# VectorE's passes in the order of their description in the FFN, and one more 7-product pair in the first group of each second product

## The chip, the cores and the metric

The kernel runs on one core of one Trainium2 chip. The metric is the device time of one execution in microseconds (us), the median of several runs. The engines' names are those of the profile: PE is the matrix engine (TensorE), PEld its weight loads, DVE is VectorE, ACT is ScalarE, POOL is GpSimd, SP the engine that issues most DMAs.

## The reference

One layer of a residual block on 256 tokens of width 2048, all in float32. The change is in the FFN, the second of three parts:

```python
merged = (sigmoid(gate_sb) * (y_sb @ w_sb_out) + sigmoid(gate_ca) * (y_ca @ w_ca_out))
x = x + merged @ w_mix_out
h = rmsnorm(x, g_ffn)
g_ff, u_ff = split(h @ w_ffn_in, 2, axis=-1)        # 2048 x 11264
x = x + (silu(g_ff) * u_ff) @ w_ffn_out             # 5632 x 2048
h = rmsnorm(x, g_ple)
x = x + sigmoid(h @ w_ple_gate) * (p @ w_ple_in)
return rmsnorm(x, g_final)
```

## The kernel before

**Every product is three products.** PE multiplies in a reduced form of float32 (`F32R`). To keep float32's precision, each operand is split: `hi` is the operand rounded, `lo` the rest, and a product is the sum of `hi*hi`, `hi*lo` and `lo*hi` (`three`, L307). Activations are split once into tables (T1, T2, T3). Weights come from memory into a `raw` buffer (128 x 1024 float32, two rows of blocks of 128 x 512); ACT casts `raw` to `hi` (L277) and DVE subtracts, `lo = raw - hi` (`minus`, L257). There are three `hi` and three `lo` buffers, a fourth of each in the FFN. PE reads them, and when its last matmul on a buffer is over, ACT may cast the next piece into it.

**Units, groups and pieces.** A *unit* computes two column groups of 512 columns side by side, with two token tiles each: four PSUM banks. Its work is cut into pieces along the contraction, two blocks of 128 rows each. A piece of one group has 12 matmuls, so both groups' pieces of the same rows have 24. Alternatively a pair of rows is done for both groups at once by a scheme with seven products in place of eight (`split_pair`, `pair_products`): 21 matmuls. The weights' sums that it needs are made of the two raw buffers by DVE (four passes of 128 x 512 into `xf` and `raw`), split by ACT (L292, L295, L298) and DVE (two `lo` passes and one of 128 x 1536). The sums of the activations come from `table_part` and `sums_of`: ACT copies the transposed tile to `af` (L496) and casts it (L500), DVE makes four small sums `fm` (L466, L257), ACT casts them (L470), DVE makes the rest.

**Which pairs, in which order.** A tuple lists a unit's pieces: a number twice is a pair of rows done plainly (one piece for each group), a negative number a 7-product pair.

```python
OUT_PAIRS = {12: (2, 3, 4), 16: (2, 4, 5, 6)}
OUT_ORDERS = {
    12: ((0, 0, 1, 1, -2, 3, 3, -4, 5, 5), (0, 0, -2, 1, -3, 1, -4, 5, 5)),
    16: ((0, 0, 1, 1, -2, 3, 3, -4, 5, 5, -6, 7, 7), (0, 0, 1, -2, 1, -4, 3, -5, 3, -6, 7, 7)),
}
```

**The FFN.** The hidden width 5632 is done in three blocks of 12, 16 and 16 tiles of 128 (blocks 0, 1, 2 below). In each block the first product (`w_ffn_in`) runs as 3, 4 and 4 units, each making 512 hidden columns; then the second product (`w_ffn_out`) runs as two units, `c = 0` (columns 0 to 1023 of x) and `c = 2` (1024 to 2047). The document calls them the first and second out unit; the change's title calls the units' pairs of columns groups. After each unit DVE adds the sums of the 7-product pairs (`mid`, L854), adds the banks (`add_sums`, L858; `add_to_sums`, L1066), multiplies (L1059), and a later task turns the result into a table (`into_table`: PE transposes L482, then `table_part`).

**Between the mixers and the FFN** the RMS norm's scale is only known after all of x: `norm`, `halve_rstd` and `broadcast` (L137, PE L139, DVE copy L140) make `p2bc`, and from then on `scale_next` multiplies each tile of T3 by it (`scale_table`, L821) after the tile's last use without it, and makes the sums for its pairs (`pair_sums`, L842). At the end of the FFN the tables for the last part are made with a gain (L508 on ACT, L509 on DVE).

**What sets the order.** `flush` goes through the pieces: `prefetch` describes the DMA and the splits of up to three pieces ahead, `products` the matmuls and what follows them, then a task. That is the order of description. The program is then put in order by a scheduler that simulates all engines: on each engine it takes what it finds ready, so the engines' queues differ from the order of description. The queues are fixed when the program is built, and an instruction that waits in one holds those that stand behind it.

Of the kernel before, what the change touches and what calls it, by code (L numbers as in the profile page):

```python
# [38 lines left out]
# [4 lines that stand above are left out]
# [10 lines left out]
def block_kernel(ctx: ExitStack, tc: tile.TileContext, x, p, w_in, w_sb_out, w_ca_out, w_mix_out,  # L53
# [100 lines left out]
    def run_task():  # L154
        name, fn = tasks.popleft()
        fn()
        if name is not None:
            done.add(name)
# [15 lines left out]
    def unit(wsrc, n0s, kts, lhs, forms, ext, slots, mid, post, needs, row0=0, pairs=PAIRS, alone=None, after=None,  # L174
             order=None, seed=None):


        if alone is None:
            state["unit"] = state.get("unit", -1) + 1
        pool = state["unit"] % 2 if alone is None else alone  # L180
        g = dict(kind="unit", post=post, mid=mid, slots=slots, after=after, lhs=lhs, keep=None, forms=forms, ext=ext, pool=pool,
                 side=1 - pool, hold=alone is not None, seed=seed)
        kts = list(kts)
        if order is None:
            order = [j for i in range(len(kts) // 2) for j in ([-i] if i in pairs and i < len(kts) // 2 - 1 else [i, i])]
        taken = [-i for i in order if i < 0]
        begun = set()
        for i in order:
            own = i < 0
            i = abs(i)  # L190
            part = kts[2 * i : 2 * i + 2]
            r = (row0 + 2 * i) * P
            src = [wsrc[r : r + 2 * P, n0 : n0 + NB].rearrange("(k p) n -> p k n", p=P) for n0 in n0s]
            pc = dict(g=g, kts=part, ncol=NB, needs=[needs(kt) for kt in part])
            if own:
                pieces.append(dict(pc, src=src, pair=True, first=i == taken[0], last=i == taken[-1]))
            else:
                b = int(i in begun)
                begun.add(i)
                pieces.append(dict(pc, src=[src[b]], block=b, first=i == 0, last=2 * i + 2 == len(kts)))  # L200
# [139 lines left out]
    def seed_next():  # L340

        pc = pieces[min(state["at"] + 2, len(pieces) - 1)]
        g = pc["g"]
        if g.get("seed") is not None and "ps" not in g:
            for b in range(2):
                open_sums(g)
                for t in range(2):
                    nc.scalar.copy(g["ps"][2 * b + t], g["seed"](b, t))

    def products(pc):  # L350
        g = pc["g"]
        if pc.get("pair"):
            pair_products(pc)
        elif g["kind"] == "unit":
            if pc["first"] and g["seed"] is None:
                open_sums(g)
            for i, kt in enumerate(pc["kts"]):
                a, z = pc["first"] and i == 0 and g["seed"] is None, pc["last"] and i == 1
                for t in range(2):
                    row_products(g["ps"][2 * pc["block"] + t], g["lhs"], kt, t, pc["hi"][:, i, :], pc["lo"][:, i, :], a, z)  # L360
            if g["after"] is not None and pc["block"] == 1:
                g["after"](pc["kts"])
            if pc["last"]:
                g["post"](g, pc["block"])
                state["hold"] = g["hold"] and pc["block"] == 0
        elif pc is pieces[1]:
            with tc.issue_after(state["mm"].ins):
                group_products(pc)
        else:
            group_products(pc)  # L370
        del pc["hi"], pc["lo"]
# [36 lines left out]
    def prefetch():  # L408
        while state["loaded"] < len(pieces) and state["raw"] + len(pieces[state["loaded"]]["src"]) <= RAW + state["places"]:
            load(pieces[state["loaded"]])  # L410
            state["loaded"] += 1
        room = 2 if state["at"] < 4 + KD // 2 else 4 if state["fourth"] is not None else 3
        while state["split"] < state["loaded"] and state["split"] <= state["at"] + 3:
            pc = pieces[state["split"]]
            if state["split"] > state["at"] and sum(map(size, pieces[state["at"] : state["split"] + 1])) > room:
                break
            behind = [started["p"]]
            if pc["g"] is pieces[4]["g"]:
                behind += started.get(pc["kts"][0] - 2, [])
            with ExitStack() as order:  # L420
                for i in behind:
                    order.enter_context(tc.issue_after(i.ins))
                split(pc)
            state["split"] += 1
# [11 lines left out]
    def flush(every=1, until=None, in_turn=False):  # L436

        n = 0
        while state["at"] < len(pieces) and (until is None or until not in done):
            pc = pieces[state["at"]]  # L440
            prefetch()
            products(pc)
            seed_next()
            state["at"] += 1
            n += 1
            if tasks and every and not state["hold"] and int(n / every) > int((n - 1) / every):
                if in_turn:
                    with tc.issue_after(state["mm"].ins):
                        run_task()
                else:  # L450
                    run_task()
# [547 lines left out]
    def rooms(t):  # L999
        return [t.rearrange("p k c s -> p (k c s)")[:, o : o + 3072] for o in (0, 3072)]  # L1000
# [42 lines left out]
    def out_form(pairs):  # L1043
        return lambda kt: late["F"][1][pairs.index(kt // 2)]
# [23 lines left out]
    def residual_of(c0):  # L1068
        return lambda b, t: x_[:, t, (c0 + b) * NB : (c0 + b + 1) * NB]

    def out_unit_post(c0, last):
        def post(g, b):
            if last and c0:
                if b == 0:
                    return
                with tc.issue_after(pieces[state["at"] + 3]["split"].ins):
                    for b in range(2):
                        add_to_sums(g, b, c0 + b)
                        residual_done(c0 + b, "ple")
                next_tables(T1, c0 + b, 32, "ple", g["pool"])  # L1080
                done.add("ffn end")
                return
            add_to_sums(g, b, c0 + b)
            if last:
                if b == 1:
                    next_tables(T1, c0 + b, 32, "ple", g["pool"])
                residual_done(c0 + b, "ple")
        return post

    k0 = 0  # L1090
    for blk, nk in enumerate(FF_BLOCKS):
        key = f"h{blk}"
        for c in range(nk // 4):
            j = k0 // 4 + c
            unit(w_ffn_in[0], (j * NB, D_FF + j * NB), range(KD), T3, lambda kt: late["F"][0][kt // 4 - 1], rooms(T1),
                 C_slots, mid, (in_post if j else first_post)(T2, c, key, OUT_PAIRS[nk]), lambda kt: ("ffn", kt),
                 pairs=PAIRS if j else (), after=None if j else scale_next)
        last = blk == len(FF_BLOCKS) - 1
        for c in (0, 2):
            unit(w_ffn_out[0], (c * NB, (c + 1) * NB), range(nk), T2, out_form(OUT_PAIRS[nk]), rooms(T3 if last else T1),  # L1100
                 C_slots, mid, out_unit_post(c, last), lambda kt, key=key: (key, kt), row0=k0,
                 order=OUT_ORDERS[nk][c // 2], seed=residual_of(c))
        k0 += nk

    pins, ple = {}, {}
# [83 lines left out]
        group("row", w_ple_gate[0], c * NB, range(KD), T1, ple_post(c), needs=pneed)  # L1189
    group("row", w_ple_gate[0], 3 * NB, range(KD), T1, last_post, needs=pneed, keep=keep)  # L1190
    state["ps"] = late["ps"][state["unit"] % 2 == 0]
    flush(until="ffn end")

    ple["pi"] = lp.tile([P, 2, NT, NB], F32, tag="C", name="pi")
    gf = ple["gf"] = lp.tile([P, D], F32, tag="gf", name="gf")
# [26 lines left out]
```

## Time and profile before

| | |
|---|---|
| median of 3 runs | 1456.49 us (1455.96 to 1457.09) |
| the profiled execution | 1455.66 us, its span 1453.9 us |
| granted TensorE clock, mean | 0.998 |
| the mixers' out products end, mix units | about 600 to 660 us |
| FFN: first products of block 0, 1, 2 | about 660 to 797, 857 to 1027, 1109 to 1279 us |
| FFN: second products of block 0, 1, 2 | about 797 to 857, 1027 to 1109, 1279 to 1359 us |
| last part and end | 1359 to 1454 us |

The stages' bounds are those at which the passes that end a unit (L966, L1059, L1066) stand in the trace. In rows of the timeline the columns are start, length, engine, line, operation, out<-in and count, then the idle time before it and what ended that. `T` stands for any of the tables, since buffer numbers are left out.

### The profile page before, as it was taken

How to read it: one execution, taken by the hardware profiler on the slowest of the kernel's cores; microseconds unless marked ns; L12 is line 12 of the kernel's file. 1: busy time of each engine (PE TensorE's matmuls, PEld its weight loads, DVE VectorE, ACT ScalarE, POOL GpSimd, SP SyncE). 2: the span in 40 equal slices, each digit the busy share in tenths (PEclk: the TensorE clock that was granted, in tenths of full speed). 3: DMA queues.
4: the chain of work that ended last, by engine and by line, in shares of the span. 5: the costliest groups of instructions: out<-in, count | busy, mean ns of one | idle time of the engine just before them, and what ended most of it. 6: DMA issues, size and time to landing. Idle time of an engine off the chain costs nothing.

```text
span 1453.9 us, 18702 instructions
## 1 busy us (share of the span) xinstructions
PE 1443.5 (99%) x6837; PEld 1208.8 (83%) x6837; DVE 1249.7 (86%) x1587; ACT 829.6 (57%) x993; POOL 25.1 (2%) x44
## 2 busy tenths in 40 slices
PE   9999999999999999999999999999999999999997
PEld 7888888888888888888888888888888888888886
DVE  6979777898987767888999999999999989999785
ACT  6456555655545665555556655566655556666652
POOL 0200000000010000000000000000000000000100
PEclk9999999999999999999999999999999999999999
DMA  9866555666675655765666666666666666665871
GB/s 319 283 189 212 181 172 172 180 205 198 199 257 164 180 168 181 231 204 173 198 192 189 196 222 194 199 201 208 193 194 216 195 186 201 215 189 178 275 230 70
DMA packets 164731, 291.17 MB, mean 200 GB/s; under 512 B 9024, under 2 KB 42096, under 8 KB 164384
## 3 DMA queue, kind: packets, MB, share of 16 engines
q1 hardware_dynamic: 162528, 281.32, 62.0%
q0 software_dynamic: 2112, 8.68, 1.8%
q8 instruction: 53, 0.87, 0.2%
q14 instruction: 38, 0.31, 0.1%
HBM read 284.19 MB, written 5.77 MB: 199 GB/s over the span
## 4 chain that ended last, share of the span: by engine, by line
PE 96%; DVE 2%; DMA 1%; issue 1%; ACT 0%; DVEq 0%; SPq 0%; ACTq 0%
PE mm L307 67%; PE su L307 13%; PE mm L392 8%; PE mm L394 4%; PE tp L482 1%; DVE lo L257 1%; DMA raw<-in_w_in 1%; PE mml L307 0%; DMA raw<-in_w_ple_in 0%; PE mm L382 0%; PE xps L536 0%; DVE xf L257 0%; PE yp L709 0%; ACT hi L277 0%; PE wt L800 0%
## 5 line engine op out<-in xcount | busy, mean ns | idle before, releaser
L307 PE MATMUL mm<-hi,T 128*128 128x512 f32 x2650 | 854.6, 391 | 0.4 <-DVE v L854 0.4
L257 DVE TENSOR_TENSOR lo<-raw,hi 128x1024 fp32r<-128x1024 f32 (+1 forms) x517 | 625.1, 1221 | 121.9 <-ACT hi L277 113.0
L277 ACT CAST hi<-raw 128x1024 fp32r<-128x1024 f32 (+1 forms) x379 | 396.7, 1050 | 381.0 <-PE mm L307 257.8
L307 PEld LDWEIGHTS mm<-hi,T 128*128 128x128 f32 x2650 | 497.3, 188 | 103.0 <-issue 0.8
L307 PE MATMUL mm<-lo,T 128*128 128x512 f32 x1325 | 517.1, 391 | 0.0
L307 PEld LDWEIGHTS mm<-lo,T 128*128 128x128 f32 x1325 | 248.9, 188 | 50.7
L392 PE MATMUL mm<-T,hi 128*128 128x512 f32 x512 | 179.8, 398 | 0.0
L394 PE MATMUL mm<-T,lo 128*128 128x256 f32 x512 | 139.7, 280 | 0.0
L295 ACT CAST hi<-raw 128x1024 fp32r<-128x1024 f32 x69 | 72.7, 1053 | 76.2 <-DVE raw L257 29.5
L257 DVE TENSOR_TENSOR T<-xf,T 128x1536 fp32r<-128x1536 f32 x61 | 107.2, 1757 | 8.0 <-ACT T L298 7.2
L392 PEld LDWEIGHTS mm<-T,hi 128*128 128x128 f32 x512 | 94.6, 188 | 20.1
L257 DVE TENSOR_TENSOR xf<-raw 128x512 f32<-128x512 f32 x138 | 95.1, 689 | 13.2 <-DMA raw<-in_w_ffn_out 4.1
L394 PEld LDWEIGHTS mm<-T,lo 128*128 128x128 f32 x512 | 96.7, 189 | 2.3
L298 ACT CAST T<-xf 128x1536 fp32r<-128x1536 f32 x61 | 90.2, 1479 | 12.7 <-DVE xf L257 12.3
L292 ACT CAST hi<-raw 128x1024 fp32r<-128x1024 f32 x69 | 72.6, 1052 | 31.0 <-PE mm L307 20.5
L307 PE MATMUL mm<-T,T 128*128 128x512 f32 (+1 forms) x279 | 77.2, 371 | 0.0
L307 PE MATMUL su<-hi,T 128*128 128x512 f32 x170 | 66.1, 394 | 0.0
L307 PEld LDWEIGHTS mm<-T,T 128*128 128x128 f32 x279 | 49.3, 188 | 9.1
L854 DVE TENSOR_TENSOR C<-su,C 128x512 f32<-128x512 f32 x72 | 47.8, 686 | 0.4
L257 DVE TENSOR_TENSOR xf<-raw,xf 128x512 f32<-128x512 f32 x69 | 47.5, 689 | 0.5
L257 DVE TENSOR_TENSOR raw<-raw 128x512 f32<-128x512 f32 x69 | 47.5, 689 | 0.4
L307 PE MATMUL su<-T,FP 128*128 128x512 f32 x174 | 47.3, 389 | 0.0
(280 smaller groups left out, 1242.7 us busy)
## 6 DMA issues: line engine op xcount, KB each, us to landing
raw<-in_w_ffn_in SPq DMA_DIRECT2D x176, 512.0 KB, 4.1
raw<-in_w_in SPq DMA_DIRECT2D x160, 512.0 KB, 4.4
raw<-in_w_ffn_out SPq DMA_DIRECT2D x88, 512.0 KB, 4.4
raw<-in_w_mix_out SPq DMA_DIRECT2D x32, 512.0 KB, 4.6
raw<-in_w_ple_gate SPq DMA_DIRECT2D x32, 512.0 KB, 4.9
raw<-in_w_sb_out SPq DMA_DIRECT2D x16, 512.0 KB, 3.8
raw<-in_w_ca_out SPq DMA_DIRECT2D x16, 512.0 KB, 4.5
x<-in_x SPq DMA_DIRECT2D x4, 512.0 KB, 10.2
```

Source lines behind the costliest of these rows:

```text
L257: return nc.vector.tensor_tensor(out, a, b, ALU.subtract)
L277: state["cast"] = nc.scalar.copy(hi[:, c : c + m], raw[:, c : c + m])
L292: nc.scalar.copy(h1, raw1)
L295: nc.scalar.copy(h2, raw2)
L298: nc.scalar.copy(xh, xf)
L307: state["mm"] = nc.tensor.matmul(ps, u, v, start=first, stop=last, skip_group_check=True)
L392: nc.tensor.matmul(ps, hi[:, i, f], lhs[:, kt, :, :].rearrange("p c s -> p (c s)"), start=a, stop=False)
L394: nc.tensor.matmul(ps[:, :S], lo[:, i, f], lhs[:, kt, 0, :], start=False, stop=z)
L482: nc.tensor.transpose(ps[:, k, t * P : (t + 1) * P], src[:, t, (k0 + k) * P : (k0 + k + 1) * P], ident)
L854: nc.vector.tensor_tensor(C[i], q, C[j], ALU.add)
```

## The change

Two edits. The first out unit of each block takes the tuple that the second has, with one 7-product pair more (three in place of two in block 0, four in place of three in blocks 1 and 2). And DVE's queue is kept in the order of description from the last pieces before the FFN to the task that ends it; PE, ACT, POOL and SP are still ordered by the scheduler.

```diff
             unit(w_ffn_out[0], (c * NB, (c + 1) * NB), range(nk), T2, out_form(OUT_PAIRS[nk]), rooms(T3 if last else T1),
                  C_slots, mid, out_unit_post(c, last), lambda kt, key=key: (key, kt), row0=k0,
-                 order=OUT_ORDERS[nk][c // 2], seed=residual_of(c))
+                 order=OUT_ORDERS[nk][1], seed=residual_of(c))
...
-    flush(until="ffn end")
+    with tc.manual_schedule(engines={mybir.EngineType.DVE}):
+        flush(until="ffn end")
```

PE has 9 matmuls of 128 x 512 fewer; DVE has 12 passes of 128 x 512 and 3 of 128 x 1536 more; ACT has 3 casts of 128 x 1536 more.

**Place 1: DVE where the FFN's norm becomes known.** `T` is T3, `lo` the rest of a weight piece, `fm` the small sums. Before:

```order
L140 COPY p2bc<-rps 128x256
L821 TENSOR_TENSOR T_5123<-T_5123,p2bc 128x2x256 x3
L257 TENSOR_TENSOR lo<-raw,hi 128x1024
L821 TENSOR_TENSOR T_5123<-T_5123,p2bc 128x2x256 x3
L257 TENSOR_TENSOR lo<-raw,hi 128x1024
L821 TENSOR_TENSOR T_5123<-T_5123,p2bc 128x2x256 x2
L842 TENSOR_TENSOR af<-T_5123 128x512
L257 TENSOR_TENSOR lo<-raw,hi 128x1024
```

Now, on the same engine and at the same place:

```order
L140 COPY p2bc<-rps 128x256
L257 TENSOR_TENSOR lo<-raw,hi 128x1024 x2
L821 TENSOR_TENSOR T_5123<-T_5123,p2bc 128x2x256 x6
L842 TENSOR_TENSOR af<-T_5123 128x512
L466 TENSOR_TENSOR fm<-af 128x128
L257 TENSOR_TENSOR fm<-af 128x128
L257 TENSOR_TENSOR fm<-fm,af 128x128
L257 TENSOR_TENSOR fm<-af,fm 128x128
L257 TENSOR_TENSOR FP<-fm,FP 128x512
L821 TENSOR_TENSOR T_5123<-T_5123,p2bc 128x2x256 x2
L257 TENSOR_TENSOR lo<-raw,hi 128x1024 x2
```

Where a `lo` pass stood after at most three scalings, eight scalings and a pair's sums stand now between the second and the third `lo` pass. On ACT, the casts of the sums (L470 into FP, for which DVE's FP passes wait) stood apart before, the second of them behind three more casts of weights. They stand together now, still behind six casts of weights, each of which waits for PE to free its buffer:

```order
L508 ACTIVATE T_5123<-tp,gT 128x256
L277 CAST hi<-raw 128x1024 x6
L470 CAST FP<-fm 128x512 x2
L277 CAST hi<-raw 128x1024 x3
L1036 ACT_TABLE_LOAD
```

**Place 2: the table of two pairs in a first product.** This is the last unit but one of blocks 1 and 2 and the last of block 0. `T_72` is T2's part, `af` the transposed tile, `fm` its sums, which end in T1's room and in F_more. DVE before, from the first table's rest to the second's end:

```order
L257 TENSOR_TENSOR T_71<-fm,T_71 128x512
L257 TENSOR_TENSOR xf<-raw 128x512
L257 TENSOR_TENSOR T_72<-af,T_72 128x2x256
L257 TENSOR_TENSOR lo<-raw,hi 128x1024
L466 TENSOR_TENSOR fm<-af 128x128
L257 TENSOR_TENSOR fm<-af 128x128
L257 TENSOR_TENSOR raw<-raw 128x512
L257 TENSOR_TENSOR lo<-raw,hi 128x1024
L257 TENSOR_TENSOR fm<-fm,af 128x128
L257 TENSOR_TENSOR xf<-raw 128x512
L257 TENSOR_TENSOR lo<-raw,hi 128x1024
```

DVE now:

```order
L257 TENSOR_TENSOR T_71<-fm,T_71 128x512
L257 TENSOR_TENSOR T_72<-af,T_72 128x2x256
L466 TENSOR_TENSOR fm<-af 128x128
L257 TENSOR_TENSOR fm<-af 128x128
L257 TENSOR_TENSOR fm<-fm,af 128x128
L257 TENSOR_TENSOR fm<-af,fm 128x128
L257 TENSOR_TENSOR F_more<-fm,F_more 128x512
L257 TENSOR_TENSOR lo<-raw,hi 128x1024 x2
```

And ACT now, at the same place; the second row waits for a matmul that is 19 matmuls ahead of the first that reads DVE's next `lo`:

```order
L277 CAST hi<-raw 128x1024
L292 CAST hi<-raw 128x1024
L470 CAST T_71<-fm 128x512
L496 COPY af<-tp 128x512
L500 CAST T_72<-af 128x2x256
L470 CAST F_more<-fm 128x512
```

DVE's three `lo` passes inside the table's work have moved behind it, and DVE's first row waits for ACT's third, which stands behind two casts of weights.

**Place 3: DVE at the start of block 0's first out unit.** The banks `mm` of the last unit of the first product are added and multiplied (L858, L1059), and the first pair of the out unit is made (`xf`, `raw`, `T_71`; the table's rest is `T_72<-af`). Before:

```order
L858 TENSOR_TENSOR C<-mm_6505,C 128x512
L858 TENSOR_TENSOR C<-mm_6521,C 128x512
L858 TENSOR_TENSOR C<-mm_6520,C 128x512
L257 TENSOR_TENSOR lo<-raw,hi 128x1024
L257 TENSOR_TENSOR T_71<-xf,T_71 128x1536
L257 TENSOR_TENSOR lo<-raw,hi 128x1024
L1059 SCALAR_TENSOR_TENSOR C<-C,r_ffn 128x512 x2
L257 TENSOR_TENSOR xf<-raw 128x512
L257 TENSOR_TENSOR lo<-raw,hi 128x1024 x2
L257 TENSOR_TENSOR raw<-raw 128x512
L257 TENSOR_TENSOR lo<-raw,hi 128x1024
L257 TENSOR_TENSOR xf<-raw 128x512
```

Now:

```order
L858 TENSOR_TENSOR C<-mm_6523,C 128x512
L1059 SCALAR_TENSOR_TENSOR C<-C,r_ffn 128x512 x2
L257 TENSOR_TENSOR xf<-raw 128x512
L257 TENSOR_TENSOR raw<-raw 128x512
L257 TENSOR_TENSOR xf<-raw 128x512
L257 TENSOR_TENSOR xf<-raw,xf 128x512
L257 TENSOR_TENSOR lo<-raw,hi 128x1024 x2
L257 TENSOR_TENSOR T_71<-xf,T_71 128x1536
L257 TENSOR_TENSOR lo<-raw,hi 128x1024
L257 TENSOR_TENSOR T_72<-af,T_72 128x2x256
L466 TENSOR_TENSOR fm<-af 128x128
L257 TENSOR_TENSOR fm<-af 128x128
```

The `lo` passes that stood among L1059 and the pair's four sums have moved behind them, in twos.

## The prediction

> **What bounds the kernel now.** First the page's busy times and its chain of work that ended last:
>
> ```profile
> PE 1443.5 (99%) x6837; PEld 1208.8 (83%) x6837; DVE 1249.7 (86%) x1587; ACT 829.6 (57%) x993; POOL 25.1 (2%) x44
> PE 96%; DVE 2%; DMA 1%; issue 1%; ACT 0%; DVEq 0%; SPq 0%; ACTq 0%
> ```
>
> PE is the bound and stands still almost nowhere. So a matmul saved is worth its full time, and a wait put into PE costs its full time too. The second view is the busy time by stretch of the FFN (columns: bounds, length, then busy us and count of PE, PEld, DVE, ACT, POOL, then the granted clock, DMA's share, GB/s). The stretches are block 0's end of the first product and its out units, then block 1's out units:
>
> ```profile
> core 0: us, PE busy (x) PEld busy (x) DVE busy (x) ACT busy (x) POOL busy (x), PEclk, DMA share, GB/s
> 795.00:825.00 30.00, 30.00 (x138) 24.84 (x137) 28.51 (x38) 20.29 (x24) 0.00 (x0) 1.00 0.62 196
> 825.00:857.00 32.00, 32.00 (x143) 26.52 (x142) 30.91 (x36) 15.54 (x16) 0.00 (x0) 1.00 0.61 200
> 984.00:1027.00 43.00, 43.00 (x196) 35.71 (x195) 41.47 (x55) 27.68 (x32) 0.00 (x0) 1.00 0.63 195
> 1027.00:1066.00 39.00, 39.00 (x177) 32.32 (x176) 36.09 (x45) 24.47 (x28) 0.00 (x0) 1.00 0.63 193
> ```
>
> PE is busy in every microsecond, and DVE has only 3 to 7% of these stretches free. The third view, the waits by kind (idle us, count, longest), tells which way the engines lead each other:
>
> ```profile
> ACT hi L277 <- PE mm L307: 257.8, 156, 6.7
> DVE lo L257 <- ACT hi L277: 113.0, 118, 2.4
> ```
>
> ACT waits until PE frees a `hi` buffer, then casts, and DVE follows on its heels. How far they run ahead of PE is therefore set by the three or four buffers: a wait inside DVE's queue can last until the next `lo` is due on PE, and no longer.
>
> **The change part by part.** I take start-to-start times ("pitch") from the timeline. PE's matmul, first and last of five starts in a row:
>
> ```profile
> 805.48 0.39 PE L307 MATMUL mm<-hi,T 128*128 128x512 f32 x1
> ...
> 806.39 0.39 PE L307 MATMUL mm<-hi,T 128*128 128x512 f32 x1
> ```
>
> (806.39 - 805.48) / 4 = 0.227 us. *What is saved:* three more 7-product pairs make 21 matmuls of 24 each, 9 fewer: 9 x 0.227 = **-2.04 us**, on the path.
>
> *What is added* is 12 DVE passes of 128x512 and 3 of 128x1536, and three casts of 128x1536 on ACT. DVE's pitches, from back-to-back passes near block 1's end:
>
> ```profile
> 990.82 0.29 DVE L466 TENSOR_TENSOR fm<-af 128x128 f32<-128x128 f32 x1
> 991.02 0.28 DVE L257 TENSOR_TENSOR fm<-af 128x128 f32<-128x128 f32 x1
> ...
> 995.16 1.76 DVE L257 TENSOR_TENSOR T<-xf,T 128x1536 fp32r<-128x1536 f32 x1
> 996.83 1.22 DVE L257 TENSOR_TENSOR lo<-raw,hi 128x1024 fp32r<-128x1024 f32 x1
> 997.97 0.69 DVE L257 TENSOR_TENSOR T<-fm,T 128x512 fp32r<-128x512 f32 x1
> 998.57 0.69 DVE L257 TENSOR_TENSOR xf<-raw 128x512 f32<-128x512 f32 x1
> ```
>
> That is 0.20 us for a `fm`, 1.67 for 128x1536, 1.14 for a `lo`, 0.60 for 128x512. So 12 x 0.60 + 3 x 1.67 = 12.2 us of DVE work are added, 4.1 in each first out unit. These stretches have 1 to 3 us of DVE free each, so the cover is about gone. ACT's pitches, and the hops between engines:
>
> ```profile
> 993.24 1.48 ACT L298 CAST T<-xf 128x1536 fp32r<-128x1536 f32 x1
> 995.00 1.06 ACT L277 CAST hi<-raw 128x1024 fp32r<-128x1024 f32 x1 [0.28 <-PE mm L307]
> 995.95 0.62 ACT L470 CAST T<-fm 128x512 fp32r<-128x512 f32 x1
> 996.47 0.58 ACT L496 COPY af<-tp 128x512 f32<-128x512 f32 x1
> 997.08 0.62 ACT L500 CAST T<-af 128x512 fp32r<-128x512 f32 x1
> ```
>
> ```profile
> 806.66 0.29 DVE L257 TENSOR_TENSOR fm<-af,fm 128x128 f32<-128x128 f32 x1
> 806.98 0.63 ACT L470 CAST F_more<-fm 128x512 fp32r<-128x512 f32 x1
> 808.43 0.39 PE L307 MATMUL mm<-hi,T 128*128 128x512 f32 x1
> 808.86 1.06 ACT L277 CAST hi<-raw 128x1024 fp32r<-128x1024 f32 x1 [1.25 <-PE mm L307]
> ```
>
> A weight cast takes 0.95, L470 0.52, L496 to L500 0.61; DVE's last sum to ACT's cast 0.03; from the start of PE's last matmul on a buffer to ACT's cast into it 0.43.
>
> *What is moved* is the large part. In the order of description, DVE may meet a pass whose input ACT makes only behind a cast that waits for PE, while PE soon needs the `lo` behind that pass. For each such loop I add up the way from PE's releasing matmul through ACT and DVE to the `lo`, and compare it with the matmuls that PE has until it needs that `lo`. What is over is PE's idle time. In before's order no loop is that tight, in accord with PE's full stretches.
>
> **A, the norm (Place 1).** Before, its rows are
>
> ```profile
> 674.82 0.60 PE L139 MATMUL rps<-dg,ones 128*128 128x256 f32 x2
> ...
> 675.46 0.42 DVE L140 COPY p2bc<-rps 128x256 f32<-128x256 f32 x1 [0.81 <-PE rps L139]
> ...
> 675.92 1.90 DVE L821 TENSOR_TENSOR T<-T,p2bc 128x512 fp32r<-128x512 f32 x3
> ...
> 677.73 1.22 DVE L257 TENSOR_TENSOR lo<-raw,hi 128x1024 fp32r<-128x1024 f32 x1
> ...
> 678.87 1.89 DVE L821 TENSOR_TENSOR T<-T,p2bc 128x512 fp32r<-128x512 f32 x3
> ```
>
> From the broadcast's start, L140 begins at 0.64 and takes 0.46; the `lo` behind it ends at 2.33, and PE needs it after its two broadcasts and four matmuls, at 1.58: 0.8. Then come a `lo` (1.14), six scalings (6 x 0.60), L842 (0.60) and the `fm` (0.80), to 8.4; the cast of FP (L470), which on ACT stands behind a weight cast that is released at 7.1 + 0.43, starts at 8.5 and ends at 9.1; FP's pass, two scalings and the `lo` end at 12.2. PE wants that `lo` at 7.8: 4.4. The next pair of rows, with the same steps but fewer scalings, lacks 0.8. Together **+6.0**.
>
> **B, the two-pair tables (Place 2), three times:** 0.43 + weight cast 0.95 + L470 0.52 + L496 0.61 + L500 and hop 0.65 + DVE's T pass 0.60 + four `fm` 0.89 + hop 0.03 + L470 and hop 0.65 + F pass 0.60 + `lo` and hop 1.26 = 7.2 us, against 19 matmuls, 4.3. PE stands 2.9 us, so **+8.6**.
>
> **C, the start of the out units (Place 3).** In block 0, from the sums that end the first product (four L854) to the next pair's `lo` DVE has 32 passes: 19 of 128x512 (11.4), two L1059 (0.66 each, 1.3), six `lo` (6.8), one of 1536 (1.7), four `fm` (0.8), in all 22.0. PE has 89 matmuls and 8 transposes of 0.11 for them, 21.1. With PE's start (0.35), the wait for the cast of F_more (0.9) and the hop (0.1), 2.3 is over, and another 0.3 by the second out unit. The casts of this unit, `hi`, 128x1536 and then DVE's 128x1536 (4.7 us against 16 to 19 matmuls, 3.6 to 4.3), lack 0.9, 0.4 and 0.6: 4.5 for block 0. The same account gives 3.2 for block 1, whose table comes with fewer sums, and 1.5 for block 2: **+9.2**.
>
> **D, the gain tables in block 2's second out unit:**
>
> ```profile
> L508 ACT ACTIVATE T<-tp,gT 128x256 fp32r<-128x256 f32 x32 | 13.6, 475 | 6.8 <-DVE T L509 5.2 <-PE tp L482 1.6
> L509 DVE SCALAR_TENSOR_TENSOR T<-tp,gT,T 128x256 fp32r<-128x256 f32 x32 | 14.0, 483 | 0.5 <-ACT T L508 0.4
> ```
>
> Now DVE's eight L509 stand together ahead of the next pair's sums, and between ACT's last L508 there are two weight casts, each waiting for PE. Each way, 0.43 + 0.95 + L508 0.51 + L509 0.52 = 2.4, stands against 8 and then 4 matmuls (1.8, 0.9): 0.6 + 1.5. The next pair's four sums and `lo`, 6.0 us after the second release, are wanted after 9 matmuls and the stall, at 3.5: 2.4. **+4.5**. **E**, one-pair tables of the units between: 0.2 twice, **+0.4**.
>
> **Sum:** 6.0 + 8.6 + 9.2 + 4.5 + 0.4 - 2.0 = +26.7. Against the profiled execution's 1455.66 (0.83 below the median of the runs, within their spread) this is **1482 us**. The loops' unknown is how much of each wait the buffers still hide. Bounds from rows: nothing hidden that I counted, and a further hop or two per loop, which I did not count (some 20 loops by 0.25 us: 1487); or ACT's casts running one buffer earlier, 4 matmuls (0.9 us) less in each of the 12 larger loops: 1472.
>
> PE would stand in gaps of 1.5 to 4.4 us. What the clock does then is shown only at the end, where PE's last matmul ends near 1445.4:
>
> ```profile
> 1445.00:1448.00 3.00, 0.38 (x4) 0.18 (x2) 1.61 (x6) 2.21 (x4) 0.00 (x0) 0.96 0.00 0
> 1448.00:1451.00 3.00, 0.00 (x0) 0.00 (x0) 1.38 (x4) 0.56 (x1) 0.00 (x0) 0.50 0.64 230
> ```
>
> A mean of 0.96 over 3 us is 1.00 until 0.24 us before the window's end and 0.50 then (0.04 x 3 / 0.5): the clock is at half 2.4 us after PE stops (1447.8 - 1445.4). The Trainium skill, "TensorE: Matmul & The Clock Gate", section "Part 1: The HAM clock gate", says that a free-running window of about 3.4 us decides: one idle window halves the clock, one busy window gives it back. By that rule a short gap costs nothing, and a gap with a full window in it about 1.7 us more (an estimate from the page's window); the trace's fall after 2.4 us is earlier than a full 3.4.
>
> **The rivals.** *1. The clock falls too.* For: the rows just shown, with gaps of 2.4 us or more at A, at B and in D. Against: before has no gap in mid-stream. If the return takes as long as the fall, each costs half of 2.4 us: 1.2. One to four of them: 1483 to 1487, with the bound above up to 1492. *2. ACT's waits are hidden,* and only A and DVE's plain excess of work (2.3 in C) stay: 1455.7 + 6.0 + 2.3 - 2.0 = 1462, with E, D's last part and block 1's share up to 1466. For: ACT's idle time is 43%. Against: its casts wait for PE, not for work. *3. Faster:* DVE and ACT hold so much lead that the loops close in it, and only the 9 matmuls stay: 1453.6. It decides if the lead of `lo` over PE is over 4.4 us at A, the largest loop. For: ACT's waits for PE last 1.7 us on average and up to 6.7, time in which it has nothing to do. Against: they are waits for the very buffers that limit the lead. *4. Losses as small as the gain,* within 0.2%, which is 2.9 us and about what a measurement of this kernel can tell from no change. That the queue isn't reordered is no case: the rows of Places 1 to 3 show it.
>
> **How the numbers follow.** The forecast 1482 (its own range 1472 to 1488) has 0.65, rival 1 0.18, rival 2 0.12, rival 3 0.03, rival 4 0.02. The range 1468 to 1490 leaves out rivals 2 to 4 and the far end of rival 1. Slower holds the forecast, 1 and 2: 0.95; same 0.02; faster 0.03.
>
> **What would show it.** PE's idle time by stretch: 6 us behind the norm's broadcast, with DVE's FP pass or a `lo` as releaser; 2.9 us in each two-pair table, released by a `lo`; some 4 us in block 0's first out unit; 4 in block 2's second. PE should have 9 matmuls fewer; a granted clock under 1.00 in mid-FFN would show rival 1. PE idle under 10 us in all would prove the loops wrong: rival 2 or 3.

## The result, and the profile after

The changed kernel takes 1502.16 us (median of 4 runs, 1501.62 to 1504.12) beside 1456.22 for the kernel before: a ratio of 1.0318, 95% interval 1.0305 to 1.0331. It is 45.9 us slower. The forecast was 1482, with a range up to 1490: the way was right, the size was not. One execution of all those reported here, of gaps_filled below, took 3571.84 us and is left out of its median.

The profiled execution took 1502.04 us, its span 1500.1, that is 46.2 more than before. Its page has these busy times:

```profile
PE 1460.9 (97%) x6828; PEld 1210.1 (81%) x6828; DVE 1276.8 (85%) x1602; ACT 834.8 (56%) x996; POOL 24.7 (2%) x44
```

PE has its 9 matmuls fewer (6828 for 6837), and is busy 17 us longer all the same: part of its matmuls were slower. That is the first sign that the clock took part. The waits by kind, of the changed kernel:

```profile
ACT hi L277 <- PE mm L307: 191.5, 126, 6.6
ACT hi L295 <- DVE raw L257: 139.5, 48, 5.4
...
DVE lo L257 <- ACT hi L277: 89.6, 88, 2.4
...
PEld mm L307 <- DVE lo L257: 18.9, 11, 4.9
...
PE mm L307 <- DVE lo L257: 15.0, 6, 4.5
```

ACT's cast L277 waits less for PE than before (191.5 us for 257.8). ACT now waits 139.5 us in its cast L295 for DVE's sum into the second raw buffer (29.5 before), and PE itself waits for `lo`.

Where does PE lose the time? The next table takes the starts of PE's matmuls from the trace and gathers, by place, what the distance between two starts has over the usual 0.227 us. What lies in a stretch of half clock is counted apart. The kernel before has about 1.5 us of such idle time in all these places; it is subtracted.

| place | forecast | PE idle | half clock |
|---|---|---|---|
| before the norm (mix pieces) | 0 | 1.1 | 0 |
| A, the norm | 6.0 | 5.7 | 2.4 |
| B, two-pair tables, three times | 8.6 | 10.6 | 3.1 |
| C, out units | 9.2 | 13.9 | 1.4 |
| D, gain tables | 4.5 | 4.0 | 3.0 |
| E, one-pair tables | 0.4 | 1.0 | 0 |
| elsewhere | 0 | 0.6 | 0 |
| sum | 28.7 | 36.9 | 9.9 |

36.9 + 9.9 - 2.0 for the matmuls saved is 44.8; the other 1.4 of the 46.2 are differences under 0.04 us each, spread over thousands of matmuls.

**A in the rows.** The timeline of the changed kernel behind the norm, of DVE, ACT and PE:

```profile
685.29 2.35 DVE L257 TENSOR_TENSOR lo<-raw,hi 128x1024 fp32r<-128x1024 f32 x2
687.55 3.69 DVE L821 TENSOR_TENSOR T<-T,p2bc 128x512 fp32r<-128x512 f32 x6
691.28 0.69 DVE L842 TENSOR_TENSOR af<-T 128x512 f32<-128x512 f32 x1
692.01 0.29 DVE L466 TENSOR_TENSOR fm<-af 128x128 f32<-128x128 f32 x1
...
691.92 1.05 ACT L277 CAST hi<-raw 128x1024 fp32r<-128x1024 f32 x1 [1.67 <-PE mm L307]
693.07 0.62 ACT L470 CAST FP<-fm 128x512 fp32r<-128x512 f32 x1
...
693.72 0.69 DVE L257 TENSOR_TENSOR FP<-fm,FP 128x512 fp32r<-128x512 f32 x1 [0.69 <-ACT FP L470]
694.33 1.29 DVE L821 TENSOR_TENSOR T<-T,p2bc 128x512 fp32r<-128x512 f32 x2
695.53 2.35 DVE L257 TENSOR_TENSOR lo<-raw,hi 128x1024 fp32r<-128x1024 f32 x2
...
696.80 0.80 PE L307 MATMUL mm<-lo,T 128*128 128x512 f32 x1 [4.47 <-DVE lo L257]
697.40 0.63 PE L307 MATMUL mm<-hi,T 128*128 128x512 f32 x1
697.82 0.63 PE L307 MATMUL mm<-lo,T 128*128 128x512 f32 x1
```

This is the loop of the forecast, pass by pass. PE stands 4.5 us for the `lo` at 695.53 (4.4 forecast). Then its matmuls start 0.42 us apart, where 0.227 is usual: the granted clock is 0.50 there, as the windows below show.

**B in the rows.** The table in block 0's third unit, from the weight cast that PE releases to the `lo` that PE waits for:

```profile
768.48 1.06 ACT L292 CAST hi<-raw 128x1024 fp32r<-128x1024 f32 x1 [0.30 <-PE mm L307]
769.80 0.63 ACT L470 CAST T<-fm 128x512 fp32r<-128x512 f32 x1 [0.27 <-DVE fm L257]
770.33 0.58 ACT L496 COPY af<-tp 128x512 f32<-128x512 f32 x1
770.94 0.62 ACT L500 CAST T<-af 128x512 fp32r<-128x512 f32 x1
...
771.59 0.69 DVE L257 TENSOR_TENSOR T<-af,T 128x512 fp32r<-128x512 f32 x1 [0.45 <-ACT T L500]
...
773.25 0.62 ACT L470 CAST T<-fm 128x512 fp32r<-128x512 f32 x1 [1.69 <-DVE fm L257]
...
774.51 2.35 DVE L257 TENSOR_TENSOR lo<-raw,hi 128x1024 fp32r<-128x1024 f32 x2
...
775.78 0.50 PE L307 MATMUL mm<-lo,T 128*128 128x512 f32 x1 [3.26 <-DVE lo L257]
```

The chain is as forecast, except for its second row: L470 starts 1.32 us after L292, not 0.95, since it waits for DVE's sums of the pair before, which end 0.37 us too late for it. The idle time is 3.4 us in all three tables, with a tail of 0.1.

**C in the rows.** Block 0's first out unit:

```profile
816.98 0.68 DVE L257 TENSOR_TENSOR xf<-raw 128x512 f32<-128x512 f32 x1
817.70 0.69 DVE L257 TENSOR_TENSOR raw<-raw 128x512 f32<-128x512 f32 x1
818.42 0.69 DVE L257 TENSOR_TENSOR xf<-raw 128x512 f32<-128x512 f32 x1
...
818.42 1.05 ACT L295 CAST hi<-raw 128x1024 fp32r<-128x1024 f32 x1 [2.68 <-DVE raw L257]
...
819.52 0.50 PE L307 MATMUL mm<-hi,T 128*128 128x512 f32 x1 [1.42 <-ACT hi L295]
```

PE stands here not for `lo`, which the forecast followed, but for the cast of the second raw buffer. That cast needs DVE's second sum, and PE reads it earlier than the `lo`. The same wait of 1.4 us stands at 1063.9, 1326.0 and 1373.2, the last one in D.

**The clock in the rows.** The windows view of the changed kernel, in stretches of 3.41 us (PE busy is the second number, the granted clock the one after POOL):

```profile
691.21:694.62 3.41, 1.12 (x5) 0.58 (x4) 2.62 (x8) 1.67 (x2) 0.00 (x0) 1.00 0.06 25
694.62:698.03 3.41, 1.23 (x3) 1.03 (x4) 3.41 (x5) 0.00 (x0) 0.00 (x0) 0.50 0.10 8
698.03:701.44 3.41, 3.41 (x9) 2.64 (x9) 2.73 (x7) 0.54 (x1) 0.00 (x0) 0.50 0.84 278
773.12:776.53 3.41, 0.75 (x3) 0.66 (x4) 2.73 (x4) 0.62 (x1) 0.00 (x0) 1.00 0.00 0
776.53:779.95 3.42, 3.42 (x9) 2.66 (x9) 3.32 (x6) 1.32 (x2) 0.00 (x0) 0.50 0.91 277
779.95:783.36 3.41, 3.41 (x16) 2.76 (x15) 3.41 (x3) 3.01 (x3) 0.00 (x0) 1.00 0.38 127
1015.49:1018.91 3.42, 1.73 (x8) 1.11 (x6) 2.26 (x7) 1.36 (x3) 0.00 (x0) 1.00 0.00 0
1018.91:1022.32 3.41, 1.84 (x8) 1.53 (x9) 3.38 (x5) 0.00 (x0) 0.00 (x0) 1.00 0.19 25
1022.32:1025.73 3.41, 3.41 (x17) 2.81 (x16) 3.34 (x5) 2.41 (x2) 0.00 (x0) 1.00 0.74 282
```

The clock falls at 694.62 and at 776.53, the second time after PE has already started again at 775.78. It stays at half for two stretches, or for one. At 1016.8 PE stands just as long as at 772 (3.42 us), but the idle time falls into two stretches, each about half busy (1.73 and 1.84 of 3.41), and the clock stays. The trace has five such falls in mid-kernel: 694.62, 776.53, 820.91, 1281.71 and 1373.87. They lie at multiples of 3.413 us from each other (24, 37, 172 and 199).

### The profile page after: what moved, and what is told of

The parts are those of the page before. It is cut to its first block, busy times and chain, and to the rows that moved or that the text cites. A ratio compares the mean times of both kernels' runs of the same rounds, so it can differ in the third digit from the quotient of the medians.

```text
span 1500.1 us, 18758 instructions
## 1 busy us (share of the span) xinstructions
PE 1460.9 (97%) x6828; PEld 1210.1 (81%) x6828; DVE 1276.8 (85%) x1602; ACT 834.8 (56%) x996; POOL 24.7 (2%) x44
## 5 line engine op out<-in xcount | busy, mean ns | idle before, releaser
L307 PE MATMUL mm<-hi,T 128*128 128x512 f32 x2610 | 842.8, 393 | 6.5 <-ACT hi L295 5.6
L277 ACT CAST hi<-raw 128x1024 fp32r<-128x1024 f32 (+1 forms) x373 | 391.3, 1052 | 318.5 <-PE mm L307 191.5
L295 ACT CAST hi<-raw 128x1024 fp32r<-128x1024 f32 x72 | 75.9, 1054 | 167.2 <-DVE raw L257 139.5
L394 PE MATMUL mm<-T,lo 128*128 128x256 f32 x512 | 139.5, 280 | 0.0
L257 DVE TENSOR_TENSOR T<-xf,T 128x1536 fp32r<-128x1536 f32 x64 | 112.3, 1755 | 16.0 <-ACT T L298 15.8
L257 DVE TENSOR_TENSOR xf<-raw 128x512 f32<-128x512 f32 x144 | 99.3, 690 | 7.3 <-DMA raw<-in_w_mix_out 2.5
L298 ACT CAST T<-xf 128x1536 fp32r<-128x1536 f32 x64 | 94.9, 1482 | 8.4 <-DVE xf L257 8.4
L292 ACT CAST hi<-raw 128x1024 fp32r<-128x1024 f32 x72 | 75.9, 1054 | 42.1 <-PE mm L307 29.3
L307 PE MATMUL su<-hi,T 128*128 128x512 f32 x178 | 70.9, 400 | 0.0
```

Source lines behind the costliest of these rows:

```text
L257: return nc.vector.tensor_tensor(out, a, b, ALU.subtract)
L277: state["cast"] = nc.scalar.copy(hi[:, c : c + m], raw[:, c : c + m])
L292: nc.scalar.copy(h1, raw1)
L295: nc.scalar.copy(h2, raw2)
L298: nc.scalar.copy(xh, xf)
L307: state["mm"] = nc.tensor.matmul(ps, u, v, start=first, stop=last, skip_group_check=True)
```

## The experiments

All times are medians; ratios are against the kernel before, run on the same chip beside each.

| kernel | us | ratio | 95% interval |
|---|---|---|---|
| tuple alone (order_alone) | 1461.98 | 1.0039 | 1.0027 to 1.0052 |
| queue alone (queue_alone) | 1493.04 | 1.0253 | 1.0239 to 1.0267 |
| norm left to the scheduler (norm_free) | 1492.63 | 1.0243 | 1.0229 to 1.0257 |
| tables left to it (tables_free) | 1491.75 | 1.0243 | 1.0227 to 1.0258 |
| tail left to it (tail_free) | 1495.83 | 1.0272 | 1.0258 to 1.0286 |
| all three left to it (three_free) | 1475.28 | 1.0130 | 1.0113 to 1.0147 |
| scalings spread (norm_spread) | 1501.60 | 1.0318 | 1.0304 to 1.0332 |
| idle times filled (gaps_filled) | 1505.20 | 1.0329 | 1.0311 to 1.0348 |
| pairs late, scheduler's queue (order_late) | 1463.98 | 1.0054 | 1.0041 to 1.0066 |
| sums ahead (sums_ahead) | 1507.70 | 1.0350 | 1.0335 to 1.0366 |

**1. Each edit alone.** First the changed kernel without its second edit (the diffs of parts 1 to 4 and 6 start from the changed kernel, that of part 5 from the kernel before):

```diff
-    with tc.manual_schedule(engines={mybir.EngineType.DVE}):
-        flush(until="ffn end")
+    flush(until="ffn end")
```

> The first out units have their third or fourth 7-product pair; DVE's queue is left to the scheduler as before. Theory of the loops (time is lost where DVE's queue in the order of description stands before a pass whose input comes late): no loop is tight here, so the 9 matmuls saved show, 1456.2 - 2.0 = 1454, unless DVE's free time (1 to 3 us in each of these units against 4.1 us of new work) is overdrawn by 1 to 2 us in each: then 1457 to 1460. Rival (the new pairs themselves cost most of the 46 us): 1480 or more.

Measured 1461.98, beyond the 1460 of the first theory: the tuple alone is no gain but costs 5.6 us. The trace has 7.4 us of idle time more than before and 2.0 us of matmuls fewer. Most of it lies in seven places. Five are alike, 0.93 us each, at the last pair of a unit: in block 0's second out unit (843.6) and in both out units of blocks 1 and 2 (1055.2, 1097.0, 1308.5, 1353.6). The other two, 0.9 and 0.85 us, are where PE goes over to the second out unit in blocks 0 and 2 (822.5 and 1318.4). So PE waits in first out units, which were changed, and as long in second ones, which were not and had no such wait before. A reading that fits, not tested by itself, is that DVE's new work eats up its lead and PE pays for part of it a unit later. The place in block 0's second unit, in the timeline of this kernel:

```profile
841.77 0.69 DVE L257 TENSOR_TENSOR raw<-raw 128x512 f32<-128x512 f32 x1
...
842.49 1.06 ACT L295 CAST hi<-raw 128x1024 fp32r<-128x1024 f32 x1 [1.27 <-DVE raw L257]
843.45 1.99 ACT L277 CAST hi<-raw 128x1024 fp32r<-128x1024 f32 x2
...
844.54 0.50 PE L307 MATMUL mm<-hi,T 128*128 128x512 f32 x1 [0.21 <-ACT hi L277]
```

It is the way through L295 again: DVE's sum is late, ACT's casts queue behind it, PE waits for a cast. The same wait in block 1's first unit, at the pair whose sums are in `F_last` (DVE adds that unit's banks, L1066, from 1062.8 to 1070.5):

```profile
1055.53 0.40 PE L307 MATMUL su<-hi,F_last 128*128 128x512 f32 x1
1056.14 0.50 PE L307 MATMUL mm<-hi,T 128*128 128x512 f32 x1 [0.21 <-ACT hi L277]
```

Next the changed kernel without its first edit:

```diff
-                 order=OUT_ORDERS[nk][1], seed=residual_of(c))
+                 order=OUT_ORDERS[nk][c // 2], seed=residual_of(c))
```

> DVE's queue in the order of description, with the old tuple for the first out units. Theory of the loops: the norm (5 us and 2.3 of low clock), the two-pair tables (10.5 and 3 of low clock), and block 2's second out unit (4 and 3 of low clock) stay, and the start of the out units loses part of its 14.5 us, since each first out unit has 4.1 us less work for DVE: 1456 + 28 to 38 = 1484 to 1494. Rival (the new pairs cost most): 1460 to 1465.

Measured 1493.04, inside the first theory's range: most of the loss is the queue's. A, B with E, and D have the idle times of the changed kernel (5.7, 11.8 and 4.2 us) and there are five falls of the clock. The first out units have only 0.4 us each, where the changed kernel has 4.1, 2.9 and 2.9, and the tuple alone 0.3, 1.2 and 1.2: most of what C costs there needs both edits. The two edits alone add up to 36.6 + 5.6 = 42.2 us, the two together cost 45.9.

**2. One place at a time left to the scheduler.**

```diff
+    flush(until=("h0", 0))
     with tc.manual_schedule(engines={mybir.EngineType.DVE}):
         flush(until="ffn end")
```

> As the changed kernel, but DVE's queue is left to the scheduler until the first unit of the FFN is over, that is over the place where the norm becomes known. Theory of the loops: the idle times there (0.66 and 4.4 us) and the stretch of half clock behind them (2.3 us) go, 1502.2 - 7.5 = 1494.7, and the idle times at the other places stay as they are. Rival (PE loses that time at the next tight place): 1500 to 1502.

Measured 1492.63 (1488.84 to 1493.48): 9.5 us less than the changed kernel, 2 more than forecast. In the trace A's idle time and its stretch of half clock are gone, and the idle times at B, C and D stand as they were, within 0.5 us at each. What A gave back is not lost again at the next places.

```diff
-    with tc.manual_schedule(engines={mybir.EngineType.DVE}):
-        flush(until="ffn end")
+    for own, key in ((True, ("h0", 3)), (False, ("h0", 7)), (True, ("h1", 7)), (False, ("h1", 11)), (True, ("h2", 7)),
+                     (False, ("h2", 11)), (True, "ffn end")):
+        with tc.manual_schedule(engines={mybir.EngineType.DVE}) if own else ExitStack():
+            flush(until=key, extra=0 if own else 4)
```

(`extra` is the number of pieces that `flush` still does after its end is reached.)

> As the changed kernel, but DVE's queue is left to the scheduler around the three two-pair tables, from the table before them to four pieces behind them. Theory of the loops: the three idle times of 3.4 us with their tails (10.5 us) and the low clock behind them (1.6 us at two of three in the profile) go: 1502.2 - 10.5 - 3.1 = 1488.6. Rival (DVE as a whole is too slow in these units, so the time is lost a little later): 1497 to 1502.

Measured 1491.75, 10.4 us less, where 13.6 were expected. The three idle times of 3.4 us are gone. But the first out units, which come next, lose more than before: 5.8, 3.6 and 3.7 us in place of 4.1, 2.9 and 2.9, with the clock falling in all three. It may be that DVE and ACT caught up a little for what follows while PE stood at the tables; no run shows that apart.

```diff
     with tc.manual_schedule(engines={mybir.EngineType.DVE}):
-        flush(until="ffn end")
+        flush(until=("h2", 15))
+    flush(until="ffn end")
```

> As the changed kernel, but DVE's queue is left to the scheduler from the second unit's beginning of block 2's second products on (from the task that makes the last table of block 2's hidden part). Theory of the loops: the idle times of block 2's out units (2.9 and 4.4 us) shrink to what the tuple alone costs there (0.2 and 3.3 us in the kernel with the tuple alone), and 3.0 us of half clock go: 1502.2 - 2.7 - 1.1 - 3.0 = 1495.4. Rival (the tail's losses are carried over from earlier): 1502.

Measured 1495.83, where 1495.4 was forecast, but the terms came out otherwise. Block 2's first out unit keeps 2.4 us of idle time of 2.9 in the changed kernel, its second 1.8 of 4.7, and the clock does not fall there. The expectation had 2.7 us less in the first and 1.1 in the second, since it put the idle time of the tuple alone at 0.2 and 3.3 us there; by unit it is 1.2 and 2.3. That the sum fits is in part luck.

> As the changed kernel, with DVE's queue left to the scheduler at the norm, around the two-pair tables and from block 2's last table on, all three at once; the order of description stays in the rest of the first products and at the start of the out units of blocks 0 and 1. If the places add up: 1502.2 less 9.6 (norm free), 10.4 (tables free) and 6.3 (tail free) gives 1475.9. If a loss that is taken away comes back at the start of the out units, as it partly did with the tables free: 1477 to 1484.

The edit is the three just shown together. Measured 1475.28: they add up, 26.9 us for 26.2 of the three alone (9.5 + 10.4 + 6.3). What is left of the queue's loss is the start of the out units of blocks 0 and 1 (3.8 and 3.4 us, each with a fall of the clock, 1.6 and 2.9 us), beside the tuple's own. Block 2's first out unit has 4.1 us of idle time, where tail_free has 2.4 and the tuple alone 1.2: there some of the loss came back, though the sum does not show it.

**3. Is A one chain?**

```diff
-        while unscaled and "p2" in done:
-            kts = unscaled.pop(0)
+        for kts in unscaled[:2] if "p2" in done else ():
+            unscaled.remove(kts)
```

> As the changed kernel, but behind the norm at most two weights' rows of T3 (four scalings) are scaled per piece, not all that have gathered. Theory of the loops: the chain of passes ahead of the late piece is 2 to 4 scalings shorter, so the idle time of 4.4 us there falls to 2.0 to 3.2, the half clock behind it (2.35 us) may not come: 1497 to 1501. Rival (the cast of FP behind a weight cast on ACT sets the end whatever stands ahead of it): 1502.

Measured 1501.60, no gain. The idle time of 4.4 us became three of 0.9, 2.2 and 1.5: A's idle time in all rose to 6.8 us, without a fall of the clock there, and the clock fell instead at block 1's table. The time is the rival's (1502), its reason only in part. At each pair DVE does stand for the cast of the sums (L470), 0.94, 0.69 and 0.69 us, and the next `lo` follows behind DVE's own pass on them and two scalings (at the third, none). But only the first of these casts starts right behind a weight cast on ACT (694.54, then 695.50); the other two wait for DVE's own small sums. What follows is that A is not bound by one long row of scalings: in a queue of fixed order, each pair's sums, with their way to ACT and back, stand ahead of `lo` passes that PE needs first, however the scalings are cut.

**4. Does idle time make the clock fall, and is there room?** In `three`, ahead of the marked piece's first product with `lo` (`zero` are 32 columns of zeros; the sum is not changed):

```diff
+            if v is lo:
+                for _ in range(state["pad"]):
+                    nc.tensor.matmul(ps[:32, :], zero, hi, start=False, stop=False, skip_group_check=True)
+                state["pad"] = 0
```

> As the changed kernel, with 52 more matmuls that add zero to an open bank: 16 ahead of the weight piece that is late behind the norm, 12 ahead of the piece that is late behind each two-pair table. They are 52 x 0.227 = 11.8 us of work for PE. Theory (PE is idle there, and the half clock behind it comes from the idle time): the matmuls fit into the idle time and cost nothing, and the half clock at the norm (2.35 us) and at the tables (1.57 us at two of three) does not come: 1502.2 - 5.5 = 1496.7, with a granted clock of 1.00 at these four places. Rival (the half clock has another cause): 1502. Rival (no room in the loops): 1508 to 1514.

The forecast of the time failed, 1505.20, while that of the clock held at all four places. The windows around the norm's wait and around block 0's table, in this kernel:

```profile
691.00:697.50 6.50, 5.78 (x26) 3.69 (x25) 5.71 (x11) 1.67 (x2) 0.00 (x0) 1.00 0.07 28
697.50:701.00 3.50, 3.50 (x17) 2.90 (x16) 3.40 (x8) 1.05 (x1) 0.00 (x0) 1.00 0.73 237
769.00:776.50 7.50, 7.04 (x32) 4.50 (x30) 5.61 (x14) 3.40 (x5) 0.00 (x0) 1.00 0.07 27
776.50:781.00 4.50, 4.50 (x20) 3.73 (x21) 4.40 (x6) 2.04 (x3) 0.00 (x0) 1.00 0.66 208
```

PE ends its waits there at nearly the same time as without the added matmuls (697.15 and 776.47, in the changed kernel 696.80 and 775.78), its idle time is down from 4.4 and 3.4 us to 0.9 and 0.6, and the clock is 1.00 throughout. At the tables the 12 matmuls fit entirely: 2.7 us of work for 2.8 us of idle time each. But A got two new waits of 0.9 and 1.0 us, and the first out units lost 6.4, 3.9 and 3.6 us (4.1, 2.9 and 2.9 without), with new falls of the clock in two of them. In all PE idles 5.3 us less than in the changed kernel and loses 2.4 us less at half clock, against 11.8 us of added matmuls. PE's order is the scheduler's, and it had moved transposes and matmuls at and behind these places too; how much of the 8.5 us between forecast and time that makes was not separated. So this run shows what makes the clock fall, not a gain in time.

**5. Where the tuple's cost comes from.**

```diff
-    12: ((0, 0, 1, 1, -2, 3, 3, -4, 5, 5), (0, 0, -2, 1, -3, 1, -4, 5, 5)),
-    16: ((0, 0, 1, 1, -2, 3, 3, -4, 5, 5, -6, 7, 7), (0, 0, 1, -2, 1, -4, 3, -5, 3, -6, 7, 7)),
+    12: ((0, 0, 1, 1, -2, -3, -4, 5, 5), (0, 0, -2, 1, -3, 1, -4, 5, 5)),
+    16: ((0, 0, 1, 1, -2, 3, 3, -4, -5, -6, 7, 7), (0, 0, 1, -2, 1, -4, 3, -5, 3, -6, 7, 7)),
```

> DVE's queue left to the scheduler; the first out units have the third or fourth 7-product pair, but with their pairs as late as in the kernel before (0, 0, 1, 1, -2, -3, -4, 5, 5 and 0, 0, 1, 1, -2, 3, 3, -4, -5, -6, 7, 7). If the early place of the first pair is what the tuple alone costs (5.5 us slower, 7.4 us of idle time): 1454 to 1456. If it is the 4.1 us of DVE work that each of these units has more: 1460 to 1464, as with the tuple alone.

Measured 1463.98: it is not the early place of the first pair. What both tuples have in common is the work, 12.2 us of DVE passes in all. This one has its pairs close together, the other spreads them; neither beats the kernel before, and other orders were not run. That the work is what costs is argued by this, not shown.

**6. The way through L295.** `raw_sums` is `split_pair`'s four sums, called ahead of the task in out units when the next piece to split is a pair:

```diff
+                pc = pieces[state["split"]]
+                if pc.get("pair") and pc["g"].get("seed") is not None and "xf" not in pc:
+                    raw_sums(pc, *pc["raw"])
             if tasks and every and not state["hold"] and int(n / every) > int((n - 1) / every):
```

> As the changed kernel, but at four places in the out units (in each first out unit, and in block 2's second) DVE makes a pair's four sums of raw weights ahead of the table's passes, not behind them. The profile of the changed kernel has PE wait there 1.4 us each time for the cast of the second raw buffer (L295), which waits for DVE's sum into that buffer. Theory of the loops, mended (C and D were mis-sized since the way through L295 was left out): these four waits of 1.57 us with their tails go, the half clock behind two of them too (1.4 and 3.0 us), and the table, 2.9 us later, costs at most a part of it: 1502.2 - 6.3 - 4.4 = 1491.5, up to 1497. Rival (DVE has too much work there in any order): 1500 to 1503, with the wait at the table's sums (su by F_last or F_more) in place of the wait for L295.

Measured 1507.70, worse than the changed kernel. The four waits for L295 are gone, as the mended theory said, but longer ones stand in their place, and the clock falls six times. Of block 1's first out unit, in this kernel:

```profile
1065.90 0.39 PE L312 MATMUL mm<-T,T 128*128 128x512 f32 x1
1068.37 1.20 PE L312 MATMUL su<-T 128*128 128x512 f32 x4 [2.08 <-DVE T L257]
```

PE waits 2.1 us for the table's part that DVE now makes 2.9 us later, and as long in block 2's first unit. In block 0's first and block 2's second it waits first for ACT's cast of 128x1536 (here L303), 1.8 and 2.6 us. The rival was right on the mechanism at two of the four places, and the time lies beyond its 1503 too: in an order by hand that has the two behind each other, one of them is late.

## Why the prediction was wrong, point by point

**The bound and the sign** held. PE is the bound, nothing hides its waits, and the saved matmuls are 9. The forecast that DVE's queue in the order of description makes PE wait at the named places held at every one of them: A, B, D and E have idle times that sit at the forecast rows. Of the 20 us that the forecast is short, 9.9 are the clock, 8.2 idle time that the loops missed, most of it in C and B, and 2 are spread thinly.

**The step that failed** is the clock: it was put among the rivals, at 0.18, with a price of 1.2 us per fall, one to four falls. It fell five times and cost 9.9 us, 2.0 each. Two things were wrong in it. The condition: the forecast took the length of a gap as what decides, by the fall 2.4 us after the last matmul at the end of the kernel before. The changed kernel shows stretches on a fixed grid, in which PE is busy less than about half; idle times of 1.8 us in all are enough where they lie in one stretch (1370.45 to 1373.87, PE busy 1.63 us of 3.42), and a gap of 3.4 us is not where it lies across two. And the price: it was half of the time to fall, where the trace has the rest of one or two whole stretches at half clock, 1.4 to 3.0 us. The Trainium skill, "TensorE: Matmul & The Clock Gate", "Part 1: The HAM clock gate", has the free-running window of 3.4 us, which this trace confirms (multiples of 3.413 us), and speaks of an idle window; here windows with PE a third or even nearly half busy (1.12 of 3.41 us, 1.63 of 3.42) were enough. The estimate of 1.7 us per fall from its window was nearer to the 2.0 than the 1.2 taken. Had the falls been in the forecast at their price, it would have read 1482 + 9.9 = 1492, still 10 us short.

**C was mis-sized,** 9.2 against 13.9. The forecast followed each loop to the `lo` alone. The nearer consumer is PE's first matmul on the second `hi`, which ACT can cast (L295) only after DVE's second sum. It also took less for block 2 (1.5) than for block 1 (3.2), where both have 2.7 in the first out unit, and it ended the account of blocks 1 and 2 before their second out units (2.1 in block 1).

**B was short by 2.0:** the sums of one pair delay the cast for the next by 0.37 us, and passes that wait for the pass just ahead of them start later than the pitch taken (the last section has the numbers). **A, D** held within 0.5 us as sums, their parts less well, so part of that is luck: A's third wait (0.8) did not come, D's second was 0.8 in place of 1.5, and the first 1.4 of D's last was for L295, not for the `lo`. **E** and the mix pieces before the norm, 1.7 us together more, were not seen.

**The 12.2 us of DVE work** had no term of their own in the sum beyond C, for "the cover is about gone". With the scheduler's queue the new tuple costs 7.4 us of idle time, more than the 2.0 us of matmuls it saves. The third rival (all hidden) was wrong with either queue. The second (ACT's waits hidden) was wrong too: the rows of B and D have ACT's casts in the chain.

**What stays open:** when an idle time is removed, part of it can come back at the next tight place (tables_free, 3 us of 13.6; three_free in block 2), or not (norm_free). Why the added matmuls in gaps_filled made the out units lose more, and how much of that is PE's new order, was not settled.

## What to carry to other kernels

In a queue fixed by hand, look for passes that wait for another engine which itself waits for the bound engine, and follow every buffer that lies behind them to its first reader: the cast that is read first, not only the last product of the chain. A change that takes matmuls off the bound engine and puts the preparation on an engine with 5% to spare was worth less than nothing here (2.0 us saved, 7.4 lost), and part of its price turned up in units that it left as they were. Where PE gets idle times that can fill half of a 3.4 us stretch, add the clock to the sum, not to the rivals.

## What the runs showed of the hardware

**The clock's window.** In the profiles of the changed kernel and of its ten variants taken together, the clock fell 39 times in mid-kernel (never with the scheduler's queue throughout), always at multiples of 3.413 us from the falls before in the same run. PE's busy share in the stretch ahead of a fall was 0.00 to 0.51. At full clock there was no stretch with a share under 0.48 that was not followed by a fall, and none over 0.52 that was; between, either came. Where the grid lies differs from run to run: the gap of 3.4 us at block 1's table cost a fall in queue_alone, where one stretch held nearly all of it (PE busy 0.06 there), and none in the changed kernel. So two profiles can differ by a fall, 1.3 to 3.0 us, by chance. PE's ends are modelled in the profile, so the third digit of the share means nothing. The way back asks for more: at half clock, a stretch with PE busy 0.92 or more always ended it, one with 0.83 or less never, and between, either came.

**Passes that depend on the one ahead.** DVE's passes of 128x512 start 0.60 us apart when they are independent, but 0.72 when each has to wait for the one ahead, as the four sums above do (816.98, 817.70, 818.42): the second overwrites what the first reads, the third and fourth read what the one ahead wrote. The same two cases for `fm` of 128x128, in the changed kernel's table of block 0:

```profile
772.20 0.29 DVE L466 TENSOR_TENSOR fm<-af 128x128 f32<-128x128 f32 x1
772.40 0.29 DVE L257 TENSOR_TENSOR fm<-af 128x128 f32<-128x128 f32 x1
772.60 0.28 DVE L257 TENSOR_TENSOR fm<-fm,af 128x128 f32<-128x128 f32 x1
772.92 0.29 DVE L257 TENSOR_TENSOR fm<-af,fm 128x128 f32<-128x128 f32 x1
```

The last starts 0.32 us behind the one whose result it reads, the others 0.20.
